# A two-layer mixer and mixture-of-experts block: the loop for left-over tokens moved behind the experts' first half, and a final norm from row sums

## Chip, cores and metric

The kernel runs on 1 core of one Trainium2 chip. The metric is the device time of one execution in microseconds (us), as the median of several runs. A program of one core has no other core to wait for, so the time is the length of its own longest chain of work.

## What is computed

Two layers over 256 latent tokens and 256 context tokens of width 1024. In each layer three token mixers (attention, gated linear attention, neighbourhood attention) are merged, added to the stream and normalised; then each token is routed to 2 of 32 experts, the experts' results are added to the stream, and it is normalised again. The second layer carries the 256 latent tokens alone through its experts. Cut to the part that the change touches:

```
def layer_norm(x, g, b):            # mean and variance over the 1024 columns
    return (x - mu) * rsqrt(var + 1e-6) * g + b

y = zeros(tokens, 1024)
for token, for its 2 experts e with gates a:     # SwiGLU experts, 1024 -> 512 -> 1024
    y[token] += a * (silu(h2[token] @ w1[e]) * (h2[token] @ w3[e])) @ w2[e]
x = layer_norm(alpha * x + gate2 * y, ln2_g, ln2_b)     # the "final norm" of the layer
# the next layer begins with
h = (x - mu(x)) * rsqrt(var(x) + 1e-6) * (1 + scale1) + shift1
```

All weights are float32. The experts' weights alone are 6 MB for each of 32 experts in each of 2 layers.

## The kernel before

**Layers and stages.** `run` goes through the layers. A layer's mixers work on tiles of 128 tokens by 1024 columns (four such tiles `x` in layer 0, and for its last part two in layer 1). Then the experts run (`experts`), then a loop for left-over tokens (`overflow`), then the final norm (`final_norm`), and in layer 1 the stream is stored. Layer 1 begins with `norm_T`, which normalises the four tiles, transposes them on TensorE and splits them into a high and a low part (`hThi`, `hTlo`) for the projections; the first of these is the small product `aT`, the next the projections `pT`.

**Experts.** Token places are set out in halves of 128 rows. A half serves one expert (H), two with 64 rows each (M) or four with 32 rows each (Q): layer 0 has 14 halves in the order MQHMQHMQHMQHMM, layer 1 has 16 halves of kind M. Two halves form a pair `dp`. `front(dp)` builds one-hot matrices for a pair on VectorE (lines 1361, 1362) and gathers its tokens on TensorE (line 1384, then the gates in lines 1369 and 1371). `body` multiplies a half by w1 and w3 (line 1507), `tail` applies silu and gate (lines 1403, 1404), transposes (1407), multiplies by w2 (1415), and after the second half of a pair calls `combine`, which brings the results back to token order on TensorE (1429, 1430), multiplies them by `g2` on VectorE (1432) and adds them to the stream (1433). The order is body 0, front 1, body 1, tail 0, body 2, tail 1, front 2 and so on.

**Weights.** An expert's weights are six pieces of 1 MB, four for `body` and two for `tail`. `load` requests them on SP's queue in the order of use and takes buffers in turn: 9 buffers in layer 0 (1 `pre`, 6 `ew`, 2 `ewb`), 14 in layer 1 (6 `ew`, 4 made of spare tiles, 4 `ewb`). A request waits on SP until the buffer's last reader is done.

**Left-over tokens.** Where an expert has more tokens than its rows, `overflow` serves them in blocks of 128 in a loop whose count, `nblk`, is known on the chip alone. With these inputs it is zero in both layers: no instruction of the loop's body is in the trace. All five engines still read the count, skip the body and meet at the loop's end. The instructions of this meeting stand in the profile under line 1546; there every engine goes through waits on the counters of the other engines and of all transfers that were requested ahead of the loop.

**Order of instructions.** A scheduler orders the instructions of each stretch between loops by priority, which is their place in the program: an engine takes the first ready instruction, and a later one where the earlier isn't ready. It can't move anything across a loop. So the program before has three stretches: to the end of layer 0's experts, from there to the end of layer 1's experts, and the last norm.

Of the kernel before, what the change touches and what calls it, by code (L numbers as in the profile page):

```python
# [21 lines left out]
NL = 2  # L22
NE = 32
# [226 lines left out]
class _Prog:  # L250
# [281 lines left out]
    def norm_T(self, l, xs):  # L532

        nc = self.nc
        xh = []
        for a in range(0, 4, NT[l]):
            for t, (_, r, m) in enumerate(self.stats_all(xs[a:a + NT[l]], APN[l]), a):
                h = self.t([128, 1024], ("whi", "wlo")[t % 2] if l else "g4", name="xh")
# [860 lines left out]
    def expert_tail(self, h1, h3, gate, w2, halves, end=False):  # L1399
# [10 lines left out]
        for n in range(2):  # L1410
            y = self.ps("Y")
            m = 128 // halves
            order = [(f, i) for f in range(4) for i in range(halves)]
            for f, i in sorted(order, key=lambda x: x[1]) if end else order:
                mm(y[m * i:m * i + m, :], aT[:, 128 * f + m * i:128 * f + m * i + m], w2(f, n, i), start=f == 0, stop=f == 3)  # L1415
            ns = slice(512 * n, 512 * n + 512)
            self.split2(y, Yh[:, ns], Yl[:, ns])
        return Yh, Yl

    def combine(self, CY, T, last):  # L1420

        nc, mm = self.nc, self.nc.tensor.matmul
        for n in range(2):
            for t in range(T):
# [8 lines left out]
                (nc.vector if last and n else nc.gpsimd).tensor_tensor(self.x1[t][:, ns], self.x1[t][:, ns], tmp, op=ALU.add)  # L1433
# [10 lines left out]
    def load(self, l, us, n, js, step=2048, most=99, after=None):  # L1444
# [4 lines left out]
        for j in js:  # L1449
            for i in range(len(us)):  # L1450
# [7 lines left out]
                if n < 6 or n >= 6 + extra:  # L1458
# [4 lines left out]
                    for v in range(0, 2048, step):  # L1463
                        self.nc.sync.dma_start(x[:, v:v + step], src[:, v:v + step])
                    w[i, j] = [x[:, 512 * v:512 * v + 512] for v in range(4)]
                else:
                    w[i, j] = []
                    for v, x in enumerate(self.spare[n - 6]):
                        self.nc.sync.dma_start(x, src[:, 1024 * v:1024 * v + 1024])
                        w[i, j] += [x[:, 0:512], x[:, 512:1024]]  # L1470

    def experts(self, l, T):
# [39 lines left out]
        def tail(dp, pr, us, hs):  # L1512
            end = SPL and 2 * dp + pr == len(halves) - 1
            self.load(l, us, 2 * dp + pr, (4,))
            self.load(l, us, 2 * dp + pr, (5,), 1024 if end else 2048)
            w = self.held[2 * dp + pr]
            Y = self.expert_tail(hs[0], hs[1], gates[dp][:, pr:pr + 1],
                                 lambda f, n, i: w[i, 4 + n][f], len(us), end)
# [8 lines left out]
        for n, x in enumerate(halves):  # L1527
            if x[1] == 1 and x[0] + 1 < len(gs):
                front(x[0] + 1)
            with self.later(0 if n else FIRST):  # L1530
                held[n] = body(*x)
            if n:
                tail(*halves[n - 1], held[n - 1])
        tail(*halves[-1], held[len(halves) - 1])
    def overflow(self, l, T):

# [4 lines left out]
        nc.vector.tensor_scalar(idx0, idx0, c["pcol"][:, 0:1], 6.0, op0=ALU.add, op1=ALU.mult)  # L1541
        if l:
            nc.vector.tensor_scalar(idx0, idx0, float(l * NE * 768), None, op0=ALU.add)
        table = self.a["ew"].rearrange("l e p j w -> (l e p j) w")
        nblk = nc.values_load(self.nblk[0:1, 0:1], min_val=0, max_val=16)
        with self.tc.For_i(0, nblk, 1):  # L1546
# [3 lines left out]
            w = []  # L1550
            for j in range(6):
                ii = self.small(1, I32)
                nc.vector.tensor_scalar(ii, row, float(j), None, op0=ALU.add)
                x = self.t([128, 2048], "ew", name="ow")
                nc.gpsimd.indirect_dma_start(out=x, out_offset=None, in_=table, in_offset=bass.IndirectOffsetOnAxis(ap=ii[:, :1], axis=0))
                w.append(x)
# [10 lines left out]
            for m in range(2):  # L1567
                h = self.ps("h")
                for k in range(8):
                    mm(h, XT[:, k], w[2 * m + k // 4][:, 512 * (k % 4):512 * (k % 4) + 512], start=k == 0, stop=k == 7)  # L1570
                hs.append(h)
            Y = self.expert_tail(hs[0], hs[1], gate, lambda f, n, i: w[4 + n][:, 512 * f:512 * f + 512], 1)
            col = self.small(1)
            nc.vector.tensor_tensor(col, sel, c["pcol"][:, 0:1], op=ALU.add)
            self.combine([(self.spots(self.slot_rows(self.over, T), col, T),) + Y], T, False)
# [5 lines left out]
    def final_norm(self, l, T, lgb):  # L1581

        nc = self.nc
        x = self.x1
        g, b = lgb
        for a in range(0, T, NB[l]):
            ts = range(a, a + NB[l])
            for t, (mu, r, m) in zip(ts, self.stats_all([x[t] for t in ts], APF[l])):
                if t in FQ[l]:
                    nc.vector.scalar_tensor_tensor(x[t], x[t], mu, g, op0=ALU.subtract, op1=ALU.mult)  # L1590
                    for i in range(2):
                        s = slice(512 * i, 512 * i + 512)
                        nc.vector.scalar_tensor_tensor(x[t][:, s], x[t][:, s], r, b[:, s], op0=ALU.mult, op1=ALU.add)  # L1593
                        if l == NL - 1:
                            nc.sync.dma_start(self.out[0, 128 * t:128 * t + 128, s], x[t][:, s])
                else:
                    nc.scalar.activation(x[t], x[t], AF.Identity, bias=m, scale=r)
                    nc.vector.tensor_tensor(x[t], x[t], g, op=ALU.mult)
                    (nc.vector if t in FD else nc.gpsimd).tensor_tensor(x[t], x[t], b, op=ALU.add)
                if t < 2 and l < NL - 1:  # L1600
                    nc.sync.dma_start(self.x2[t], x[t])
        return x
# [12 lines left out]
    def run(self):  # L1615
# [7 lines left out]
        for l in range(NL):  # L1623
# [48 lines left out]
            if l:  # L1672
                lgb = self.final_loads(l)
            self.overflow(l, T)
            if l == 0:
# [4 lines left out]
                lgb = self.final_loads(l)  # L1680
            xs = self.final_norm(l, T, lgb)
# [30 lines left out]
```

## Time and profile before

| | |
|---|---|
| median of 3 runs | 2152.49 us (2150.43 to 2153.63) |
| the profiled execution, its own time | 2150.77 us |
| its span, first to last instruction | 2148.9 us |
| TensorE (PE) busy | 1973.0 us, 92% |
| VectorE (DVE) busy | 964.7 us, 45% |
| ScalarE (ACT) busy | 561.5 us, 26% |
| GpSimd (POOL) busy | 277.5 us, 13% |
| moved by DMA | 562.41 MB, mean 262 GB/s |
| mean granted TensorE clock | 0.969 |

Times in the views are us from the span's start. PE is the matmul row, PEld its weight loads; engine names with a q are the engines' queues, where branches, semaphores and transfer requests are processed. A float32 matmul stands in the trace as two records. In rows of the timeline the first number is the start, the second the length from the first to the last of the instructions that the row merges. "DMA share" is the busy share of the 16 DMA engines. Layer 0's experts use weights from about 697 to 1176, layer 1's from 1674 to 2122.

### The profile page before, as it was taken

The page shows a single profiled execution, that of the slowest core. Times are in us where ns is not written, and L with a number is a line of the kernel's source. Part 1 is how long each engine was busy: PE and PEld are TensorE (multiplying, and loading weights), DVE is VectorE, ACT ScalarE, POOL GpSimd, SP SyncE. Part 2 cuts the span into 40 slices and gives each one's busy share as a digit, 9 for nine tenths or more (in the row PEclk, how much of TensorE's full clock was granted, in tenths as well). Part 3 has the DMA queues.
Part 4 walks back from the last instruction along what each step waited for, and adds up shares of the span by engine and source line. Part 5 has one row for each costly group of instructions (what it writes and reads, how often), then busy time and mean ns, then how long its engine had stood idle before and what let it go on. Part 6 is the DMA issues. An engine that isn't in the chain of part 4 may idle for free. (4 is left out here: it accounts for less than half of the span.)

```text
span 2148.9 us, 28075 instructions
## 1 busy us (share of the span) xinstructions
PE 1973.0 (92%) x10749; PEld 1179.0 (55%) x10749; DVE 964.7 (45%) x2236; ACT 561.5 (26%) x992; POOL 277.5 (13%) x268
## 2 busy tenths in 40 slices
PE   6999999999998898989899598999996999999995
PEld 2676777767885353445253176887795433333331
DVE  4676765554487131222022766776658222221113
ACT  3453344443333000000010254444452111100000
POOL 1322100011100010111011222100020001000000
PEclk9999999999999999999999798999997999999998
DMA  8436222333328999999998723642466999999995
GB/s 300 160 118 220 69 69 70 94 99 120 99 91 321 400 420 420 372 385 420 420 369 367 276 84 116 197 127 85 140 210 253 401 421 422 422 422 422 421 422 224
DMA packets 113987, 562.41 MB, mean 262 GB/s; under 512 B 13302, under 2 KB 14838, under 8 KB 72120
## 3 DMA queue, kind: packets, MB, share of 16 engines
q1 hardware_dynamic: 113272, 558.85, 67.7%
q8 instruction: 87, 1.43, 0.3%
q10 hardware_dynamic: 576, 1.70, 0.2%
q14 instruction: 52, 0.43, 0.1%
HBM read 557.36 MB, written 3.15 MB: 261 GB/s over the span
## 5 line engine op out<-in xcount | busy, mean ns | idle before, releaser
L1507 PE MATMUL h<-ew,XT 128*64 128x512 f32 (+2 forms) x2048 | 479.0, 616 | 39.6 <-DMA ew<-in_ew_dram 39.5
L1507 PEld LDWEIGHTS h<-ew,XT 128*64 128x64 f32 (+2 forms) x2048 | 147.3, 136 | 325.7 <-issue 251.0
L1415 PE MATMUL Y<-ew,aT 128*64 128x512 f32 (+2 forms) x1024 | 250.4, 598 | 10.2 <-DMA ew<-in_ew_dram 7.8
L292 DVE TENSOR_TENSOR wlo<-raw,whi 128x1024 fp32r<-128x1024 f32 (+1 forms) x140 | 179.1, 1279 | 138.0 <-ACT whi L291 136.9
L1433 POOL TENSOR_TENSOR x<-x,ct 128x512 f32<-128x512 f32 x82 | 104.9, 1306 | 996.9 <-DVE ct L1432 873.7
L380 PE MATMUL pT<-hThi,whi 128*128 128x512 f32 (+1 forms) x576 | 204.0, 354 | 2.2 <-DVE zq L869 1.4
L291 ACT CAST whi<-raw 128x1024 fp32r<-128x1024 f32 (+1 forms) x140 | 145.4, 1039 | 223.4 <-PE pT L381 123.8
L382 PE MATMUL pT<-hThi,wlo 128*128 128x512 f32 (+1 forms) x576 | 203.2, 353 | 0.2 <-DVE wlo L292 0.2
L381 PE MATMUL pT<-hTlo,whi 128*128 128x512 f32 (+1 forms) x576 | 202.9, 352 | 0.0
L1404 DVE SCALAR_TENSOR_TENSOR act<-h,s,sl 128x512 f32<-128x512 f32 x30 | 22.5, 751 | 317.6 <-PE h L1507 263.9
L806 ACT CAST Yh<-Y 128x512 fp32r<-128x512 f32 x60 | 35.2, 586 | 467.7 <-PE Y L1415 467.7
L1415 PEld LDWEIGHTS Y<-ew,aT 128*64 128x64 f32 (+2 forms) x1024 | 75.5, 133 | 149.2 <-issue 123.8
L807 DVE TENSOR_TENSOR Yl<-Y,Yh 128x512 fp32r<-128x512 f32 x60 | 41.4, 690 | 252.8 <-ACT Yh L806 249.7
L380 PEld LDWEIGHTS pT<-hThi,whi 128*128 128x128 f32 x576 | 110.7, 192 | 23.8 <-issue 6.0
L382 PEld LDWEIGHTS pT<-hThi,wlo 128*128 128x128 f32 x576 | 110.7, 192 | 16.1 <-issue 2.6
L381 PEld LDWEIGHTS pT<-hTlo,whi 128*128 128x128 f32 x576 | 110.7, 192 | 14.3 <-issue 1.9
L380 PE MATMUL pM<-whi,hThi 128*128 128x512 f32 (+1 forms) x304 | 110.7, 369 | 3.6 <-ACT qTkT L645 1.9
L381 PE MATMUL pM<-wlo,hThi 128*128 128x512 f32 (+1 forms) x304 | 110.9, 365 | 0.0
L382 PE MATMUL pM<-whi,hTlo 128*128 128x512 f32 (+1 forms) x304 | 110.1, 364 | 0.0
L495 PE MATMUL mod<-wmod,sT 128*32 128x512 f32 x320 | 75.2, 636 | 22.5 <-DVE s L341 14.1
L1408 ACT COPY aT<-aT 128x512 f32<-128x512 f32 x30 | 17.6, 585 | 294.4 <-PE aT L1407 294.4
L1384 PE MATMUL XT<-OH,h2hi 128*128 128x256 f32 x352 | 88.6, 289 | 0.2 <-DVE OH L1362 0.2
(364 smaller groups left out, 3088.5 us busy)
## 6 DMA issues: line engine op xcount, KB each, us to landing
ew<-in_ew_dram SPq DMA_DIRECT2D x326, 1024.0 KB, 13.6
raw<-in_w_dram SPq DMA_DIRECT2D x145, 512.0 KB, 3.7
ew<-in_ew_dram SPq DMA_DIRECT2D x116, 512.0 KB, 13.5
wmod<-in_wmod_dram SPq DMA_DIRECT2D x96, 512.0 KB, 6.4
nb<-in_nb_dram SPq DMA_DIRECT2D x32, 256.0 KB, 3.8
g<-md SPq DMA_DIRECT2D x12, 256.0 KB, 7.3
row<-in_ln_dram SPq DMA_DIRECT2D x4, 512.0 KB, 5.3
lgb<-in_ln_dram SPq DMA_DIRECT2D x4, 512.0 KB, 12.2
```

Source lines behind the costliest of these rows:

```text
L291: self.nc.scalar.copy(hi, src)
L292: (eng or self.nc.vector).tensor_tensor(lo, src, hi.bitcast(F32), op=ALU.subtract)
L380: mm(out, lh, rh, start=start, stop=False)
L381: mm(out, lh, rl, start=False, stop=False)
L382: mm(out, ll, rh, start=False, stop=stop)
L495: nc.tensor.matmul(p[32 * j:32 * j + 32, :], self.sT[:, k, :], raws[j // 2][:, 512 * (j % 2):512 * (j % 2) + 512], start=k == 0, stop=k == 7)
L806: self.nc.scalar.copy(hi, src)
L807: self.nc.vector.tensor_tensor(lo, src, hi.bitcast(F32), op=ALU.subtract)
L1384: mm(p[:, w * j:w * j + w], self.h2s[t][part][:, 128 * k:128 * k + 128], OH[:, t], start=t == 0 and part == 0, stop=t == T - 1 and part == 1)
L1415: mm(y[m * i:m * i + m, :], aT[:, 128 * f + m * i:128 * f + m * i + m], w2(f, n, i), start=f == 0, stop=f == 3)
L1433: (nc.vector if last and n else nc.gpsimd).tensor_tensor(self.x1[t][:, ns], self.x1[t][:, ns], tmp, op=ALU.add)
L1507: mm(h[m * i:m * i + m, :], XTs[dp][:, k, 128 * pr + m * i:128 * pr + m * i + m], w[i, 2 * q + k // 4][k % 4], start=k == 0, stop=k == 7)
```

## The change

1. `overflow` is called inside `experts`, behind the first half's body and tail. Ahead of it stand new calls of `load` that request weights of halves 1 and 2, as many as there are buffers. `front(1)`, which is called in the same turn, now stands behind the loop. The order becomes body 0, tail 0, loop, front 1, body 1, body 2, tail 1 and so on.
2. The loop's body takes its weights in 24 pieces of 256 KB through the small `ct` buffers and no longer in six through `ew`.
3. The last half's w2 pieces, four in all, are requested in halves of 512 KB, the first halves of all four ahead of the second halves, and the w2 product no longer goes by expert first.
4. `combine` of the last pair adds on VectorE throughout (before: GpSimd for the first 512 columns, VectorE for the second) with an instruction that also returns the row sums.
5. `final_norm` takes the mean from these sums and the variance from a squaring pass on ScalarE, tile by tile, where it had bn_stats over two tiles at a time; all scaling is on VectorE. It passes on the row sums of its result, and `norm_T` of layer 1 does likewise.
6. `final_loads` (the norm's gain and offset) follows the experts in both layers.

```
         xh = []
-        for a in range(0, 4, NT[l]):
+        for t in range(4 if l else 0):
+            h, st = self.t([128, 1024], ("whi", "wlo")[t % 2], name="xh"), self.small(20)
+            nmu, v, m = (st[:, i:i + 1] for i in range(3))
+            nc.vector.tensor_scalar(nmu, self.total[t], -1.0 / 1024, None, op0=ALU.mult)
+            nc.scalar.activation(h, xs[t], AF.Square, bias=nmu, accum_out=v)
+            nc.vector.tensor_scalar(v, v, 1.0 / 1024, EPS, op0=ALU.mult, op1=ALU.add)
+            r = self.rsqrt(v, 1, st[:, 3:6])
+            nc.vector.tensor_tensor(m, nmu, r, op=ALU.mult)
+            nc.scalar.activation(h, xs[t], AF.Identity, bias=m, scale=r)
+            xh.append(h)
+        for a in range(0, 0 if l else 4, NT[l]):
...
-            order = [(f, i) for f in range(4) for i in range(halves)]
-            for f, i in sorted(order, key=lambda x: x[1]) if end else order:
+            for f, i in [(f, i) for f in range(4) for i in range(halves)]:
...
+        if last:
+            self.sums = [self.small(2) for _ in range(T)]
...
-                (nc.vector if last and n else nc.gpsimd).tensor_tensor(self.x1[t][:, ns], self.x1[t][:, ns], tmp, op=ALU.add)
+                if last:
+                    nc.vector.scalar_tensor_tensor(self.x1[t][:, ns], tmp, 1.0, self.x1[t][:, ns], op0=ALU.mult, op1=ALU.add, accum_out=self.sums[t][:, n:n + 1])
+                else:
+                    nc.gpsimd.tensor_tensor(self.x1[t][:, ns], self.x1[t][:, ns], tmp, op=ALU.add)
...
+            for _, x, src in sorted(parts, key=lambda y: y[0]) if step < 2048 else parts:
+                self.nc.sync.dma_start(x, src)
...
-            end = SPL and 2 * dp + pr == len(halves) - 1
-            self.load(l, us, 2 * dp + pr, (4,))
-            self.load(l, us, 2 * dp + pr, (5,), 1024 if end else 2048)
+            end = 2 * dp + pr == len(halves) - 1
+            self.load(l, us, 2 * dp + pr, (4, 5), 1024 if end else 2048)
...
         for n, x in enumerate(halves):
+            if n == 1:
+                tail(*halves[0], held[0])
+                free = PRE[l] + 6 + RNG[l] + len(self.spare) + 6 * len(halves[0][2])
+                for j in (1, 2):
+                    self.load(l, halves[j][2], j, range(4), most=free - self.nw)
+                self.overflow(l, T)
             if x[1] == 1 and x[0] + 1 < len(gs):
                 front(x[0] + 1)
-            with self.later(0 if n else FIRST):
-                held[n] = body(*x)
-            if n:
+            held[n] = body(*x)
+            if n > 1:
                 tail(*halves[n - 1], held[n - 1])
...
+        for t in range(T):
+            x, st = self.x1[t], self.small(20)
+            nmu, v = st[:, 0:1], st[:, 1:2]
+            nc.vector.tensor_scalar(nmu, self.sums[t][:, 0:1], self.sums[t][:, 1:2], -1.0 / 1024, op0=ALU.add, op1=ALU.mult)
+            nc.scalar.activation(junk[:, t % 2] if l else junk.rearrange("p a b -> p (a b)"), x, AF.Square, bias=nmu, accum_out=v)
+            nc.vector.tensor_scalar(v, v, 1.0 / 1024, EPS, op0=ALU.mult, op1=ALU.add)
+            r = self.rsqrt(v, 1, st[:, 3:6])
+            STT(x, x, nmu, g, op0=ALU.add, op1=ALU.mult)
+            if l == NL - 1:
+                for i in range(2):
+                    s = slice(512 * i, 512 * i + 512)
+                    STT(x[:, s], x[:, s], r, b[:, s], op0=ALU.mult, op1=ALU.add)
+                    nc.sync.dma_start(self.out[0, 128 * t:128 * t + 128, s], x[:, s])
+                continue
+            self.total.append(st[:, 6:7])
+            STT(x, x, r, b, op0=ALU.mult, op1=ALU.add, accum_out=st[:, 6:7])
...
             self.experts(l, T)
-            if l:
-                lgb = self.final_loads(l)
-            self.overflow(l, T)
             if l == 0:
                 right.close()
                 left.close()
                 self.pre.close()
                 left, right = self.mixers(1)
-                lgb = self.final_loads(l)
-            xs = self.final_norm(l, T, lgb)
+            xs = self.final_norm(l, T, self.final_loads(l))
```

## Rows read from the trace of the kernel before

**Rows 1.** Busy time by stretch: PE, PEld, DVE, ACT, POOL, clock, DMA share, GB/s

```profile
697.00:1176.00 479.00, 442.77 (x2231) 199.97 (x2227) 102.69 (x166) 38.14 (x66) 61.08 (x48) 0.98 0.98 401
1674.00:2122.00 448.00, 428.23 (x1960) 165.32 (x1956) 85.74 (x140) 43.13 (x76) 36.40 (x28) 1.00 1.01 419
```

**Rows 2.** Waits in layer 0's experts, 690 to 1190: total us, times, longest

```profile
PEld h L1507 <- DMA ew<-in_ew_dram: 58.1, 34, 3.5
```

**Rows 3.** Busy time by stretch, the seam between the layers, columns as in rows 1

```profile
1175.50:1195.00 19.50, 13.31 (x52) 6.34 (x48) 9.24 (x15) 1.17 (x2) 4.97 (x4) 0.96 0.02 6
1195.00:1235.00 40.00, 22.59 (x78) 6.08 (x79) 32.40 (x100) 14.04 (x17) 11.14 (x4) 0.68 0.97 368
```

**Rows 4.** Timeline from layer 0's last additions to layer 1's first products

```profile
1188.83 1.29 DVE L1432 TENSOR_TENSOR ct<-cb,g 128x512 f32<-128x512 f32 x2 [1.53 <-PE cb L1430]
...
1194.07 0.81 SPq L1612 DMA_DIRECT2D lgb<-in_ln_dram  x2
...
1195.34 4.84 DVE L336 BATCH_NORM_STATS2 s<-x 128x6 f32<-128x512 f32 x8 [1.62 <-issue]
...
1214.91 2.18 DVE L1599 TENSOR_TENSOR x<-x,lgb 128x1024 f32<-128x1024 f32 x1
...
1224.36 4.64 ACT L539 ACTIVATE xh<-x,s 128x1024 f32<-128x1024 f32 x4 [16.15 <-DVE s L346]
...
1243.17 0.68 DVE L292 TENSOR_TENSOR hTlo<-h,hThi 128x512 fp32r<-128x512 f32 x1
```

**Rows 5.** Timeline of the run's end

```profile
2108.71 3.65 PE L1415 MATMUL Y<-ew,aT 128*64 128x512 f32 x16 [1.32 <-DMA ew<-in_ew_dram]
...
2126.20 3.66 PE L1415 MATMUL Y<-ew,aT 128*64 128x512 f32 x12
...
2136.07 2.47 DVE L336 BATCH_NORM_STATS2 s<-x 128x6 f32<-128x512 f32 x4 [1.70 <-issue]
...
2143.21 2.73 DVE L1593 SCALAR_TENSOR_TENSOR x<-x,s,lgb 128x512 f32<-128x512 f32 x4
```

**Rows 6.** A pass of VectorE over one tile, ns

```profile
L1590 DVE SCALAR_TENSOR_TENSOR x<-x,s,lgb x2: 1267/1273/1279, 2138.7 to 2140.0; 128x1024 f32<-128x1024 f32 x2
```

**Rows 7.** Instructions of the loop's line, both layers: ns min/median/max, first and last start

```profile
L1546 DVEq EVENT_SEMAPHORE  x25: 21/50/50, 1193.8 to 2135.8; - x25
L1546 SPq EVENT_SEMAPHORE  x23: 27/28/5606, 1187.2 to 2134.5; - x23
L1546 PEldq COMPARE_BRANCH  x6: 70/182/325, 1188.0 to 2134.6; - x6
```

**Rows 8.** Busy time by stretch, the last weights, columns as in rows 1

```profile
2120.00:2125.00 5.00, 4.34 (x18) 1.28 (x19) 0.21 (x1) 0.59 (x1) 0.00 (x0) 1.00 0.31 126
```

**Rows 9.** Busy time by stretch of 2 us, layer 0, columns as in rows 1

```profile
682.00:684.00 2.00, 2.00 (x10) 1.81 (x9) 2.00 (x12) 0.00 (x0) 0.00 (x0) 0.50 1.03 415
...
696.00:698.00 2.00, 2.00 (x12) 0.71 (x10) 0.00 (x0) 0.00 (x0) 0.00 (x0) 1.00 0.46 78
718.00:720.00 2.00, 2.00 (x24) 0.60 (x20) 1.23 (x3) 0.00 (x0) 0.00 (x0) 1.00 0.26 45
720.00:722.00 2.00, 2.00 (x24) 0.55 (x17) 0.00 (x0) 0.00 (x0) 0.00 (x0) 1.00 0.80 287
```

**Rows 10.** Timeline of PE, layer 0, the gather between halves 0 and 1

```profile
706.39 0.39 PE L1384 MATMUL XT<-OH,h2hi 128*128 128x256 f32 x1
...
715.17 7.91 PE L1507 MATMUL h<-ew,XT 128*32 128x512 f32 x66
```

**Rows 11.** Timeline of DVE, one-hot matrices of four tiles

```profile
716.41 1.67 DVE L1362 SCALAR_TENSOR_TENSOR OH<-cst,s,O 128x256 fp32r<-128x256 f32 x4
```

**Rows 12.** Timeline of PE, layer 1, the gather between halves 0 and 1

```profile
1683.35 0.39 PE L1384 MATMUL XT<-OH,h2hi 128*128 128x256 f32 x1
...
1687.81 12.67 PE L1507 MATMUL h<-ew,XT 128*64 128x512 f32 x58
```

**Rows 13.** The page's transfer requests: KB each, us from issue to landing

```profile
raw<-in_w_dram SPq DMA_DIRECT2D x145, 512.0 KB, 3.7
```

More of the change, by code (lines that the diff above doesn't have):

```diff
@@ L535, in norm_T @@
         xh = []
-        for a in range(0, 4, NT[l]):
+        for t in range(4 if l else 0):
[9 more added lines that the diff above has]
+        for a in range(0, 0 if l else 4, NT[l]):
             for t, (_, r, m) in enumerate(self.stats_all(xs[a:a + NT[l]], APN[l]), a):
-                h = self.t([128, 1024], ("whi", "wlo")[t % 2] if l else "g4", name="xh")
+                h = self.t([128, 1024], "g4", name="xh")
                 nc.scalar.activation(h, xs[t], AF.Identity, bias=m, scale=r)
@@ L1397, in spots, with expert_tail @@
         return C
-    def expert_tail(self, h1, h3, gate, w2, halves, end=False):
+    def expert_tail(self, h1, h3, gate, w2, halves):
         nc, mm = self.nc, self.nc.tensor.matmul
@@ L1449, in load @@
         for j in js:
+            parts = []
             for i in range(len(us)):
@@ L1462, in load @@
                         self.nc.gpsimd.tensor_copy(x[0:32, 0:1], after[0:32, 0:1])
-                    for v in range(0, 2048, step):
-                        self.nc.sync.dma_start(x[:, v:v + step], src[:, v:v + step])
+                    parts += [(v // step, x[:, v:v + step], src[:, v:v + step]) for v in range(0, 2048, step)]
                     w[i, j] = [x[:, 512 * v:512 * v + 512] for v in range(4)]
@@ L1468, in load @@
                     for v, x in enumerate(self.spare[n - 6]):
-                        self.nc.sync.dma_start(x, src[:, 1024 * v:1024 * v + 1024])
+                        parts.append((v, x, src[:, 1024 * v:1024 * v + 1024]))
                         w[i, j] += [x[:, 0:512], x[:, 512:1024]]
+            for _, x, src in sorted(parts, key=lambda y: y[0]) if step < 2048 else parts:
+                self.nc.sync.dma_start(x, src)
     def experts(self, l, T):
@@ L1512, in tail @@
         def tail(dp, pr, us, hs):
-            end = SPL and 2 * dp + pr == len(halves) - 1
-            self.load(l, us, 2 * dp + pr, (4,))
-            self.load(l, us, 2 * dp + pr, (5,), 1024 if end else 2048)
+            end = 2 * dp + pr == len(halves) - 1
+            self.load(l, us, 2 * dp + pr, (4, 5), 1024 if end else 2048)
             w = self.held[2 * dp + pr]
             Y = self.expert_tail(hs[0], hs[1], gates[dp][:, pr:pr + 1],
-                                 lambda f, n, i: w[i, 4 + n][f], len(us), end)
+                                 lambda f, n, i: w[i, 4 + n][f], len(us))
             col = 2 * dp + pr
@@ L1540, in overflow @@
         nc.vector.tensor_scalar(idx0, self.eb, 128.0, None, op0=ALU.mult)
-        nc.vector.tensor_scalar(idx0, idx0, c["pcol"][:, 0:1], 6.0, op0=ALU.add, op1=ALU.mult)
+        nc.vector.tensor_scalar(idx0, idx0, c["pcol"][:, 0:1], 24.0, op0=ALU.add, op1=ALU.mult)
         if l:
-            nc.vector.tensor_scalar(idx0, idx0, float(l * NE * 768), None, op0=ALU.add)
-        table = self.a["ew"].rearrange("l e p j w -> (l e p j) w")
+            nc.vector.tensor_scalar(idx0, idx0, float(l * NE * 3072), None, op0=ALU.add)
+        table = self.a["ew"].rearrange("l e p j (v w) -> (l e p j v) w", w=512)
         nblk = nc.values_load(self.nblk[0:1, 0:1], min_val=0, max_val=16)
@@ L1549, in overflow, with piece @@
             nc.vector.scalar_tensor_tensor(eq, eq, 1.0, idx0, op0=ALU.mult, op1=ALU.mult, accum_out=row)
-            w = []
-            for j in range(6):
+            def piece(j):
                 ii = self.small(1, I32)
                 nc.vector.tensor_scalar(ii, row, float(j), None, op0=ALU.add)
-                x = self.t([128, 2048], "ew", name="ow")
+                x = self.t([128, 512], "ct", name="ow")
                 nc.gpsimd.indirect_dma_start(out=x, out_offset=None, in_=table, in_offset=bass.IndirectOffsetOnAxis(ap=ii[:, :1], axis=0))
-                w.append(x)
+                return x
             d = self.small(2 * T)
@@ L1569, in overflow @@
                 for k in range(8):
-                    mm(h, XT[:, k], w[2 * m + k // 4][:, 512 * (k % 4):512 * (k % 4) + 512], start=k == 0, stop=k == 7)
+                    mm(h, XT[:, k], piece(8 * m + k), start=k == 0, stop=k == 7)
                 hs.append(h)
[L1572 to L1575, printed above, removed]
+            Y = self.expert_tail(hs[0], hs[1], gate, lambda f, n, i: piece(16 + 4 * n + f), 1)
+            p = self.ps("row")
+            for t in range(T):
+                nc.tensor.transpose(p[:, 128 * t:128 * t + 128], OH[:, t].bitcast(F32), self.ident)
+            C = self.t([128, 128 * T], "o1", F32R, "C")
+            nc.vector.tensor_copy(C, p[:, :128 * T])
+            self.combine([(C,) + Y], T, False)
             nc.vector.tensor_scalar(cnt, cnt, 1.0, None, op0=ALU.add)
@@ L1583, in final_norm @@
         nc = self.nc
-        x = self.x1
+        STT = nc.vector.scalar_tensor_tensor
         g, b = lgb
[L1586 to L1601, printed above, removed]
@@ L1602, in final_norm @@
-        return x
+        self.total = []
+        if l:
+            junk = self.t([128, 2, 1024], "e8", name="junk")
+        else:
+            junk = self.t([128, 2, 512], "g4", name="junk")
+        for t in range(T):
+            x, st = self.x1[t], self.small(20)
[13 more added lines that the diff above has]
+            STT(x, x, r, b, op0=ALU.mult, op1=ALU.add, accum_out=st[:, 6:7])
+            if t < 2:
+                nc.sync.dma_start(self.x2[t], x)
@@ L1604, in final_loads @@
+        return self.x1
     def final_loads(self, l):
```

## The prediction

> **What bounds the kernel now.** I read the page first, for the balance of engines, then busy time by stretch, then the waits, and last the timeline at the three places that the change touches. The stretches show two stages in which transfers set the pace: while the experts run, the DMA engines are busy 0.98 of the time in layer 0 and all of it in layer 1, at 401 and 419 GB/s [rows 1]. At 419 GB/s a piece of 1 MB (1.049 million bytes) takes 2.5 us. TensorE looks busy there too, but in layer 0 it waited for weights 34 times, 58.1 us in all [rows 2], and the ends of its matmuls are modelled. So a time without transfers, while weights are still to come, delays the end by as much. It is otherwise between the layers: nothing moves from 1175.5 to 1195, as SP stands at the loop, and then 40 us pass at 368 GB/s in which PE has 22.6 us of work [rows 3]. There a chain of VectorE and ScalarE decides: last additions, loop, statistics, norm, statistics again, `xh`, transposes [rows 4]. At the run's end it is VectorE alone [rows 5].
>
> **What the change gives back: the seam between the layers.** Before, from the first multiplication of the last additions at 1188.83 to the last `hTlo` at 1243.85 it takes 55.0 us, with 1.62 us at the loop and 4.84 us of bn_stats on the way [rows 4]. After, VectorE has for each tile a multiplication (1.29/2 = 0.65 us [rows 4]) and an addition with row sum (2.73 us for the four passes over 512 columns [rows 5], the last to its end 0.75, and some 0.07 to read the sum, an estimate), twice two passes at 1.27 us [rows 6] less their overlap (1.2 us apart), and some ten small instructions at 0.1 to 0.2 us: 1.5 + 2.5 + 1.3 = 5.3 us, for four tiles 21 us, so the last tile leaves the final norm at about 1210. Then `norm_T` needs of it a squaring pass on ScalarE (a pass over 1024 columns took 4.64/4 = 1.16 us [rows 4]), ten dependent small instructions (2 us) and the pass to `xh` (1.16): 1214.5. VectorE also does the small instructions of the three earlier tiles and the evictions of the first two tiles' transposes meanwhile, for which I add 5.5 us (an estimate): 1220. From the last `xh` to the last `hTlo` it took 14.8 us before [rows 4] (1229.0 to 1243.85) for four tiles; two of them are through by now, so 7.4 us: 1227.4, which is 16 us earlier. I take 15. The bounds: 9 us if the transposes take all 14.8 us again, 22 if the 5.5 us find gaps. The modulation weights, which cost those 40 us, can now be requested while PE finishes, since SP no longer stands at the loop (it waited 5606 ns there for the last of the engines [rows 7]); they then cost the chain nothing. If they came as late as before, PE's products would still be in the way of the transposes, which is the lower bound again.
>
> **The run's end.** The last weights land at 2121.6 (0.31 of the stretch from 2120 [rows 8]), yet the last w2 product runs from 2126.20 to 2129.86 [rows 5], as it comes behind the first 512 columns' product and combine. With the second halves of all four pieces last, only half of a product of 3.65 us [rows 5] for each column half is left after landing; I put the end at 2125.5. Four multiplications with additions, now all on VectorE, take 5.9 us from 2126.3: 2132.2, against 2134.4 (1.70 us of idle time before 2136.07 [rows 5]). From there to the last instruction's end at 2145.94 it took 11.6 us: the loop 1.7, bn_stats 2.5, the rest 7.4. The two first fall away, and a squaring pass comes in, of which little shows for the first tile and 1.3 us for the second, while the last additions' order leaves less to wait for: about 7.5 us, so 2139.7. That is 6 us; bounds 3 (products in the old order) and 8. In layer 0 the new order of the last requests gives nothing, as PE has 13.3 us of work after the last landing [rows 3]. GpSimd's additions of the first 512 columns, which VectorE takes over, fall into a stretch in which it is busy for 9.24 of 19.5 us [rows 3].
>
> **What the change costs: the loop in the middle of the weights.** The body isn't run, so its smaller pieces cost nothing. But every engine goes through waits at the loop's exit, some eleven in a loop (25 on VectorE for two loops [rows 7]), and they name the counters of all transfers requested ahead of it. Before, all weights had landed by then, and the price was 1.6 to 1.7 us [rows 4, 5]. Now nine requests in layer 0 and fourteen in layer 1 are made just ahead of the loop, and the loop ends when the last of them has landed. The stream itself isn't held until then; but at that moment every buffer is full, nothing is requested, and PE must first empty a buffer.
>
> Layer 0: transfers resume at about 697 when body 0 frees buffers [rows 9]. Three pieces of half 0 and nine more follow, 12 x 2.5 = 30 us, so the last lands at 727. Its buffer is free in time: body 0 is done at 706.4 [rows 10], silu and transposes take about 3 us, the two w2 products 2 x 3.65 us [rows 5], so 717, where the last two transfers need theirs at 722. PE then idles from 717 to the exit at 728. Queued behind the loop is first `front(1)`, by priority, then body 1. The first one-hot matrix is ready 0.9 us later (0.42 us [rows 11], as much before it). Before, the same work, from the gather's start at 706.39 [rows 10] to the transfers' return at 720.4 (share 0.26, then 0.80 [rows 9]), took 14.0 us. PE's clock comes on top: after a stretch of little work it was granted 0.50, the 1.2 GHz level, at 682 to 684 [rows 9]; four such us cost 2. So transfers resume at 745 and 18 us are lost, against 1.9 lost at the same place before [rows 9]: 16 us.
>
> Layer 1: transfers run without a gap from 1674 [rows 1]. Behind the fourteen that are there, twelve follow: the last lands at 1704, the exit is at 1705. One-hot 0.9, gather and gates 4.5 (1683.35 to 1687.81 [rows 12]), the first products, 3.65, that empty two buffers [rows 5], the clock 2, start of a transfer 0.7: 1716.7, so 13 us. After both gaps the stream goes on as before, and nothing makes the loss good: layer 1's stream has no other gap [rows 1], and layer 0's next half of four experts waits for weights anyway.
>
> The sum: 2150.77 (the profiled execution's own time, 1.7 under the median of 2152.49) + 16 + 13 - 15 - 6 = 2158.8; I say 2159.
>
> **A rule against the change.** PE's branches at the loop took 325 ns at most [rows 7], so I add nothing for the jump over the body. The Trainium skill (Runtime: NRT & Kernel Launch, section Instruction fetch mechanics) says that a taken branch whose target lies outside the instructions held has to wait until they are fetched by DMA. The trace doesn't bear this out with a long wait at the two loops of before. As a rival: a fetch at the exit in each layer on PE, priced like a small transfer on a quiet queue, 3.7 us [rows 13], gives 2159 + 7 = 2166.
>
> **Rivals.** (a) PE takes body 1 first and the gather later. Body 1's weights are ready, the one-hot matrices aren't, and an engine takes what is ready; against it, the gather went first in both layers before [rows 10, 12]. Then the gap ends after 3.65 + 2 + 0.7 us: 735 and 1711.4, a loss of 6 and 7.4, and the time is 2150.8 + 13.4 - 21 = 2143. It decides as soon as the two gaps together stay under 21 us. (b) The loop does not hold for the requested weights. The stream then covers the loop, PE's idle time is a few us of what it waits for anyway, and the time is about 2150.8 - 21 + 2 = 2132. Only the program's list of waits speaks against it, since nothing was in flight at the loops of before. (c) The seam gives nothing, because layer 1's start depends on something else than the last `xh`: 2159 + 15 = 2174. Against it: PE sat without work in front of the transposes, and ScalarE waited 16.15 us for the statistics [rows 4].
>
> **How the numbers follow.** Forecast 0.55, (a) 0.25, (b) 0.08, the jump 0.07, (c) 0.05. A difference under 0.2%, 4.3 us, is about what a measurement of this kernel can't tell from none. The forecast's own range is 2150 to 2167, from the bounds of its four terms; of its 0.55 some 0.37 lie above 2156.8 and 0.04 below 2148.2. From (a) 0.19 is faster and 0.05 the same, (b) is faster, the jump and (c) are slower. Faster 0.31, same 0.18, slower 0.51. The range for 8 in 10 leaves out (b), (c) and the tails: 2140 to 2167.
>
> **What would show it.** In the changed trace: PE idle for about 11 us after tail 0 in both layers, and no transfers for 13 to 18 us after it; line 1384 ahead of line 1507 behind the loop; semaphore waits of the loop's line that end with a landing. At the seam the modulation weights before 1195 and the first `aT` product some 15 us sooner, counted from the last addition. At the end no bn_stats. The forecast is wrong if transfers go on through the loop, if line 1507 comes first, or if the seam's chain is shortened by another amount than 9 to 22 us.

## The result, and the profile after

The changed kernel takes 2165.97 us (median of 4 runs, 2163.87 to 2168.70), the kernel before on the same chip 2151.46 us: ratio 1.0068, 95% interval 1.0050 to 1.0085, so slower by 14.5 us. The forecast was 2159, slower by 8. The profiled execution of after has a span of 2164.2 us, 15.3 more than that of before.

The table divides both spans at the same events. Landings and resumptions are read from stretches of 1 us by their DMA share, the rest from the timeline. A landing stands where the summed share ends, so the last few packets come up to 1.5 us later than its number. Each kernel has one profiled execution, which can lie some us off its median (7.2 us above it for e5_five_held).

| Stage | before | after | difference |
|---|---|---|---|
| to the transfers' return at half 0, layer 0 | 697.0 | 695.5 | -1.5 |
| from there to layer 0's last landing | 478.4 | 499.3 | +20.9 |
| to the end of layer 0's last combine on PE | 14.0 | 11.4 | -2.6 |
| to layer 1's first `pT` product | 60.9 | 47.1 | -13.8 |
| to body 0 of layer 1 | 419.1 | 419.8 | +0.7 |
| to layer 1's last landing | 451.9 | 467.3 | +15.4 |
| to VectorE's last instruction | 24.6 | 20.5 | -4.1 |

The two streams lose 36.3 us; the seam, the run's end and a shorter rest of work behind layer 0's last landing give back 20.5. The stretches of after around the loop show where the two lost (columns as in [rows 1]); layer 0's answer to [rows 9]:

```profile
714.00:716.00 2.00, 0.55 (x4) 0.00 (x0) 0.69 (x1) 0.59 (x1) 0.00 (x0) 1.00 0.99 414
...
726.00:728.00 2.00, 0.00 (x0) 0.00 (x0) 0.00 (x0) 0.00 (x0) 0.00 (x0) 0.50 0.28 115
728.00:730.00 2.00, 0.04 (x1) 0.05 (x1) 0.24 (x4) 0.00 (x0) 0.00 (x0) 0.50 0.00 0
...
744.00:746.00 2.00, 2.00 (x24) 0.65 (x20) 1.59 (x5) 0.00 (x0) 0.00 (x0) 1.00 0.00 0
746.00:748.00 2.00, 2.00 (x24) 0.65 (x20) 0.00 (x0) 0.00 (x0) 0.00 (x0) 1.00 0.35 74
...
1708.00:1710.00 2.00, 0.00 (x0) 0.00 (x0) 0.00 (x0) 0.00 (x0) 0.00 (x0) 0.50 0.34 143
1710.00:1712.00 2.00, 0.84 (x2) 0.75 (x3) 0.78 (x6) 0.00 (x0) 0.00 (x0) 0.50 0.00 0
1720.00:1722.00 2.00, 2.00 (x12) 0.68 (x10) 0.43 (x2) 0.00 (x0) 0.00 (x0) 1.00 0.00 0
1722.00:1724.00 2.00, 2.00 (x12) 0.61 (x10) 0.00 (x0) 0.00 (x0) 0.00 (x0) 1.00 0.40 61
```

PE is done with tail 0 at 714.6 and stands, while the transfers run on until 726.6 (0.28 of the stretch from 726, summed); they come back at 747.3. In layer 1 the last landing is at 1708.7, the return at 1723. Added up by their shares, the gaps cost 20.6 and 14.5 us. The instructions of the loop's line (1570 in after; first and last start) put the loop's end between landing and return, in layer 0 first, then in layer 1:

```profile
L1570 SPq EVENT_SEMAPHORE  x12: 28/28/28, 715.9 to 729.2; - x12
L1570 PEldq COMPARE_BRANCH  x3: 104/185/6066, 710.8 to 729.7; - x3
...
L1570 SPq EVENT_SEMAPHORE  x12: 28/28/28, 1698.9 to 1710.6; - x12
L1570 PEldq COMPARE_BRANCH  x3: 70/173/412, 1692.5 to 1710.9; - x3
```

SP passes its last wait at 729.2 and at 1710.6, 2.6 and 1.9 us behind the landings as the share sums them. Much of that is the stream's own end, which trickles. From 722 to 735, in 40 slices of 0.325 us, it is:

```profile
GB/s 429 454 429 429 454 429 429 403 378 403 454 378 353 126 76 76 76 25 25 0 0 0 0 0 0 0 0 0 0 25 0 0 0 0 0 0 0 0 0 0
```

The last packets of weights come at about 728.0 (the lone 25 is an instruction packet), in layer 1 at about 1709.7, so SP's last wait ends some 1 us behind them. The view of SP's waits from 712 to 735 puts 12.6 us at the loop's line down to landings of `ew`. PE's timeline behind the loop in layer 0:

```profile
729.96 0.79 PE L1440 MATMUL cb<-Yh,C 128*128 128x512 f32 x1 [15.41 <-DVE s L1503]
...
733.53 0.41 PE L1394 MATMUL XT<-OH,h2hi 128*128 128x256 f32 x1
...
742.68 3.64 PE L1525 MATMUL h<-ew,XT 128*32 128x512 f32 x32
```

Eight products of pair 0's combine come first (3.6 us, at granted clock 0.50), then the gather, and body 1 only 12.7 us behind the loop. The seam (the answer to [rows 4]):

```profile
1199.82 1.29 DVE L1443 TENSOR_TENSOR ct<-cb,g 128x512 f32<-128x512 f32 x2 [1.84 <-PE cb L1441]
...
1202.30 0.34 SPq L1648 DMA_DIRECT2D lgb<-in_ln_dram  x1
...
1203.67 17.54 SPq L493 DMA_DIRECT2D wmod<-in_wmod_dram  x10
...
1205.10 1.09 PE L1441 MATMUL cb<-Yl,C 128*128 128x512 f32 x4
...
1205.53 1.29 DVE L1443 TENSOR_TENSOR ct<-cb,g 128x512 f32<-128x512 f32 x2 [0.19 <-PE cb L1441]
...
1225.55 1.27 DVE L1635 SCALAR_TENSOR_TENSOR x<-x,s,lgb 128x1024 f32<-128x1024 f32 x1
...
1230.00 4.63 ACT L544 ACTIVATE xh<-x,s 128x1024 f32<-128x1024 f32 x4 [1.46 <-DVE s L281]
...
1244.85 2.36 DVE L292 TENSOR_TENSOR hTlo<-h,hThi 128x512 fp32r<-128x512 f32 x2
```

The row at 1199.82 is the first multiplication of the first 512 columns, the one at 1205.53 of the second; the row at 1188.83 in [rows 4] is of the second too. SP requests the norm's rows 3.9 us ahead of the last combine's end (1206.2); before it was 4.7 us behind it. From that end the last pass of the final norm takes 20.6 us to finish, the last `xh` 28.4 and the last `hTlo` 41.0, where it was 54.4.

### The profile page after: what moved, and what is told of

Read it like the earlier page. It is cut to its first block, busy times and chain, and to the rows that moved or that the text cites. A ratio compares the mean times of both kernels' runs of the same rounds, so it can differ in the third digit from the quotient of the medians.

```text
span 2164.2 us, 28127 instructions
## 1 busy us (share of the span) xinstructions
PE 1968.4 (91%) x10749; PEld 1180.1 (55%) x10749; DVE 960.3 (44%) x2275; ACT 569.4 (26%) x1008; POOL 260.2 (12%) x259
## 4 chain that ended last, share of the span: by engine, by line
PE 47%; DMA 15%; DVE 3%; ACT 2%; issue 1%; SPq 0%; DVEq 0%; ACTq 0%
DMA ew<-in_ew_dram 14%; PE h L1525 13%; PE Y L1424 9%; PE XT L1394 4%; PE cb L1440 2%; PE pT L380 2%; PE cb L1441 2%; PE pT L381 2%; PE pT L382 2%; PE pM L381 1%; PE pM L382 1%; PE pM L380 1%; PE PV L969 1%; PE PT L955 1%; PE S L1020 1%
## 5 line engine op out<-in xcount | busy, mean ns | idle before, releaser
L1424 PE MATMUL Y<-ew,aT 128*64 128x512 f32 (+2 forms) x1024 | 249.0, 598 | 11.4 <-DMA ew<-in_ew_dram 7.8
L1448 POOL TENSOR_TENSOR x<-x,ct 128x512 f32<-128x512 f32 x76 | 97.5, 1311 | 974.9 <-DVE ct L1443 974.9
L1414 DVE SCALAR_TENSOR_TENSOR act<-h,s,sl 128x512 f32<-128x512 f32 x30 | 22.5, 751 | 331.9 <-PE h L1525 277.0
L1440 PE MATMUL cb<-Yh,C 128*128 128x512 f32 x176 | 63.5, 435 | 36.4 <-DVE s L1503 30.2
## 6 DMA issues: line engine op xcount, KB each, us to landing
lgb<-in_ln_dram SPq DMA_DIRECT2D x4, 512.0 KB, 13.8
```

The lines of the kernel that those rows point to most:

```text
L1440: mm(p, C[:, 128 * t:128 * t + 128], Yh[:, ns], start=i == 0, stop=False)
L1448: nc.gpsimd.tensor_tensor(self.x1[t][:, ns], self.x1[t][:, ns], tmp, op=ALU.add)
```

## The experiments

All times are medians, ratios are to the kernel before run on the same chip in the same set, with 95% intervals. The stage times in the text are those of the table above, read from each kernel's profile.

**e1_loop_back.** The loop behind the experts, and with it body 1 ahead of tail 0 and no requests ahead of the loop; in layer 1 the norm's rows are requested ahead of it, as before. Everything else is as changed.

```diff
-            if n == 1:
-                tail(*halves[0], held[0])
-                ...
-                self.overflow(l, T)
...
-            if n > 1:
+            if n:
                 tail(*halves[n - 1], held[n - 1])
...
             self.experts(l, T)
+            if l:
+                lgb = self.final_loads(l)
+            self.overflow(l, T)
...
```

> The loop for left-over tokens stands behind the experts again, body 1 comes ahead of tail 0 and the requests ahead of the loop are gone; row sums, final norm and the order of the last requests stay as changed (the row sums leave out what the loop would add; no token is left over with these inputs). Theory: the loop in the middle of the weights cost 18.8 us of the transfers in layer 0 and 15.2 in layer 1 by the trace of the changed kernel, and its return costs some 5 us at the seam and 1.7 at the end: 2166 - 34 + 6.7 = 2139, at any rate 2134 to 2145. Rival (the row sums and the request order cost the time, not the loop's place): 2155 or more.

Measured 2136.79 us, 0.9937 (0.9914 to 0.9960). The two streams take 481.8 and 452.1 us (before 478.4 and 451.9), the seam's stage 49.3, the end 22.5. Most of the 3.4 us that layer 0's stream has more than before it has less behind the last landing (11.7 us to the last combine's end instead of 14.0). The theory holds and the rival falls: the loop's place, with the order and the requests that go with it, turns a gain of 0.6% into a loss of 0.7%.

**e2_five_less.** `free` is smaller by five in each layer.

```diff
-                free = PRE[l] + 6 + RNG[l] + len(self.spare) + 6 * len(halves[0][2])
+                free = PRE[l] + 6 + RNG[l] + len(self.spare) + 6 * len(halves[0][2]) - 5
```

> As the changed kernel, but five pieces fewer are requested ahead of the loop in each layer, so that the last one requested lands about when TensorE is done with tail 0 (714.6 and 1697). Theory (the exit waits for the landing of all that was requested ahead of it): the loop ends at about 717 and 1699, some 13 and 12 us sooner; SP then requests the other five while TensorE gathers, and of the gaps of 20.7 and 14.1 us about 7 and 3 are left: 2166 - 25 = 2141, 2137 to 2150. Rival (the loop's place costs by its joining of all engines, the fetch of instructions or the clock, whatever is in flight): ten pieces of 2.5 us come later, 2166 to 2190.

Measured 2163.16 us, 1.0057 (1.0037 to 1.0077), as the changed kernel. The experiment tells nothing of the theory: the same nine and fourteen requests go out ahead of the loop. In layer 0 SP makes twelve, three of half 0 and nine more, from 690.5 to 711.0 and the next at 741.8; in the changed kernel twelve from 694.9 to 715.5 and the next at 746.3. So the requests of body 1, which stand behind the loop in the source, moved up past it: that nothing is moved across a loop, as the section on the kernel before has it, doesn't hold for these requests. The last landings (722.0 and 1701.9) and the gaps (some 21 and 15.6 us) are those of after.

**e3_no_loop.** As e1_loop_back, without the call of `overflow` (tokens left over, of which there are none here, would get no service).

> The loop is left out altogether (no service for left-over tokens; there are none with these inputs), body 1 ahead of tail 0 as before, the rest as changed. Theory: what is left of e1_loop_back's time without 1.7 us at the end and 1.6 to 6 us at the seam: 2131 to 2136. Rival (loops cost next to nothing wherever they stand): within 2 us of e1_loop_back.

Measured 2141.10 us, 0.9949 (0.9932 to 0.9967). This lies outside both ranges. The theory's small print fell: without any loop the seam takes 49.2 us (49.3 with it) and the end 22.5 (22.5), so behind the experts the loop costs nothing that shows, with a new norm whose sums don't wait for it. The median is 4.3 us above that of e1_loop_back, but the intervals overlap, so that the two aren't told apart. In the profiled executions layer 1's stream takes 456.5 us instead of 452.1; the same 350 us of e1_loop_back, and then of e3_no_loop:

```profile
1740.00:2090.00 350.00, 330.95 (x1494) 124.74 (x1490) 67.58 (x108) 32.97 (x58) 31.24 (x24) 1.00 1.02 422
```

```profile
1740.00:2090.00 350.00, 329.58 (x1482) 124.55 (x1484) 67.57 (x108) 32.93 (x58) 31.20 (x24) 1.00 1.02 417
```

The queues are as full, but move 417 GB/s instead of 422, which over 450 us is 5 us. Why, and whether another execution of the same kernel would do so, no run here shows.

**e4_old_norm.** As changed, with the last additions, the statistics by bn_stats and the final norm of before (`combine`, `final_norm`, `norm_T`).

> As the changed kernel, with the loop in the middle and the requests ahead of it, but with the old last additions, bn_stats and final norm. Theory: the seam's gain of 13.4 us is two thirds the norm's and a third the loop's absence, and at the run's end the norm is worth 2: 2166 + 9 + 2 = 2177, 2172 to 2182. Rival (the seam gained because SP's requests no longer stand behind the loop): 2166 to 2170.

Measured 2174.95 us, 1.0111 (1.0092 to 1.0129), as the theory had it. The seam's stage takes 56.2 us: going from before over this kernel to the changed one, 4.7 of 60.9 us fall without the new norm and another 9.1 with it. At the run's end it is 21.4 against 20.5. VectorE's timeline shows what fell away at the seam:

```profile
1218.11 8.95 DVE L1611 TENSOR_TENSOR x<-x,lgb 128x1024 f32<-128x1024 f32 x4 [1.04 <-ACT x L1610]
1226.99 1.27 DVE L336 BATCH_NORM_STATS2 s<-x 128x6 f32<-128x512 f32 x2
```

**e5_five_held.** As changed, five requests made to depend on the loop (`cnt` is the loop's counter, `after` makes GpSimd write the buffer's first column from it ahead of the request).

```diff
                 for j in (1, 2):
-                    self.load(l, halves[j][2], j, range(4), most=free - self.nw)
+                    self.load(l, halves[j][2], j, range(4), most=max(0, free - 5 - self.nw))
                 self.overflow(l, T)
+                for j in (1, 2):
+                    self.load(l, halves[j][2], j, range(4), most=max(0, free - self.nw), after=self.cnt)
```

> As the changed kernel, with five of the requests really held behind the loop in each layer: their buffers' first element is written by GpSimd from the loop's counter, so that nothing can move them ahead (in e2_five_less the program's order put nine and fourteen ahead of the loop all the same). Theory (the exit waits for the landing of what was requested ahead of it): last landing before the loop at about 714 and 1696, loop ends at 717 and 1699 instead of 730 and 1711, the gaps of 20.7 and 14.1 us in the transfers shrink to about 7 and 3: 2166 - 25 = 2141, 2136 to 2150. Rival (joining all engines, instruction fetch, clock: the price does not hang on what is in flight): the exits stay where they are or the held pieces come 25 us later, 2166 to 2190.

Measured 2144.71 us, 0.9970 (0.9959 to 0.9982), 21 us less than the changed kernel, with the same work. SP's last waits at the loop, in layer 0 and in layer 1, and PE's branches:

```profile
L1575 SPq EVENT_SEMAPHORE  x12: 27/28/2999, 708.2 to 718.3; - x12
L1575 PEldq COMPARE_BRANCH  x3: 100/193/3694, 713.0 to 722.1; - x3
...
L1575 SPq EVENT_SEMAPHORE  x12: 28/28/2095, 1683.5 to 1693.7; - x12
L1575 PEldq COMPARE_BRANCH  x3: 70/181/409, 1688.2 to 1694.1; - x3
```

Counted from the transfers' return at half 0 the loop lets SP go after 20.3 us, instead of 33.7 in the changed kernel. In layer 0 two gaps are left, in the stretches of 2 us:

```profile
716.00:718.00 2.00, 0.76 (x4) 0.00 (x0) 0.58 (x1) 0.58 (x1) 0.00 (x0) 1.00 0.13 45
718.00:720.00 2.00, 0.00 (x0) 0.00 (x0) 0.18 (x2) 0.00 (x0) 0.65 (x5) 1.00 0.18 29
...
734.00:736.00 2.00, 2.00 (x29) 1.38 (x31) 0.87 (x5) 0.58 (x1) 0.00 (x0) 1.00 0.04 12
736.00:738.00 2.00, 2.00 (x24) 0.56 (x20) 1.92 (x6) 0.00 (x0) 0.00 (x0) 1.00 0.00 0
```

They cost 3.4 and 6.8 us, the second because PE still gathers when the five pieces have landed. Layer 1's costs 3.0 us.

**e6_all_held.** The same with every request of body 1 and later held behind the loop.

> The same with every request behind half 0's own held until the loop has ended. Theory: TensorE's tail 0 then sets the exit, at about 717 and 1699. In layer 0 the stream stops when half 0's last three pieces have landed (704.5) and goes on at 717: a gap of 12.5 us instead of 20.7. In layer 1 half 0's pieces have all landed at about 1674, and the gap is 25 us instead of 14.1: 2166 - 8 + 11 = 2169, 2163 to 2175. Rival (as for e5_five_held): the exits stay at 730 and 1711, gaps of 25 and 37 us, 2190 or more.

Measured 2170.90 us, 1.0104 (1.0087 to 1.0121). Now SP waits at the loop for the engines, in layer 0 for 10.8 us, in layer 1 for 26.2 us (the largest of its waits); the view of waits names VectorE, whose last work of tail 0 in layer 0 ends at 713.8, behind PE's last product at 712.4:

```profile
L1575 SPq EVENT_SEMAPHORE  x12: 28/28/10764, 697.0 to 714.0; - x12
...
L1575 SPq EVENT_SEMAPHORE  x6: 27/28/26232, 1662.4 to 1689.1; - x6
```

The gaps cost 13.7 and 29.1 us (expected 12.5 and 25). With e5_five_held and the changed kernel this makes three settings of one quantity, and the loop's end follows the later of two events in each: the last landing (the changed kernel), or the engines' end of tail 0 (here, and by a little in e5_five_held, where the last packets come at 716.7 and VectorE ends at 718.1).

**e7_layer1_only.** The loop in the middle in layer 1 only.

```diff
-            if n == 1:
+            if n == 1 and l:
```

> The loop in the middle in layer 1 only, behind the experts in layer 0 (whose row sums leave out what the loop would add; no token is left over); norm and request order as changed. Theory: e1_loop_back's 2137 plus the 15.2 us of layer 1's gap, less about 2 at the run's end: 2150, 2146 to 2154. Rival (what the second layer costs is only the delay of the first, handed on): 2137 to 2140.

Measured 2153.35 us, 1.0011 (1.0000 to 1.0022). Layer 1's stream takes 468.2 us, layer 0's 479.8: the two losses stand side by side and add up.

**e8_sums_in_loop.** As e1_loop_back, with the loop's additions writing the row sums too.

```diff
-            self.combine([(C,) + Y], T, False)
+            self.combine([(C,) + Y], T, True)
```

> As e1_loop_back, with the loop's own additions writing the row sums again, so that the norm is right with left-over tokens too. Theory: the loop's body is not entered, so this costs nothing: 2137, 2133 to 2141, faster than both kernels. Rival (the sums now wait for the loop, and the loop's exit costs the norm's start): 2141 to 2145.

Measured 2140.01 us, 0.9942 (0.9928 to 0.9955): within the range and faster than both kernels, with the service for left-over tokens complete in the program (none are left over, so it isn't exercised). But it isn't free: the trace has the rival's wait. The seam takes 50.3 us and the end 24.1, 1.0 and 1.6 more than in e1_loop_back. At the end VectorE is done with the last addition at 2126.6 and reads the row sums only behind the loop:

```profile
2128.28 0.34 DVE L1617 TENSOR_SCALAR s<-s 128x1 f32<-128x1 f32 x2 [1.71 <-issue]
```

**e9_body_first.** As changed, `front(1)` called behind body 1.

> As the changed kernel, but the second pair's gather and gates are called behind body 1, so that TensorE starts on body 1 when the loop ends. Theory (the transfers stand until TensorE has emptied a buffer, and in the changed kernel the first products of the combine and the gather go ahead of that): the transfers resume some 6.4 us behind the loop's end in each layer (first products 3.65, clock 2, start 0.7) instead of 17.4 and 12, so 11 + 5.5 us less: 2149, 2145 to 2154. Rival (the wait for the landings is the whole price, what comes first behind the loop is hidden): 2162 or more.

Measured 2155.80 us, 1.0010 (0.9995 to 1.0025), 1.8 us above the range. PE's timeline behind the loop, and the stretches of the last landing and of the return:

```profile
731.96 6.26 PE L1525 MATMUL h<-ew,XT 128*32 128x512 f32 x32 [15.29 <-DVE s L1503]
738.15 0.50 PE L1440 MATMUL cb<-Yh,C 128*128 128x512 f32 x1
```

```profile
728.00:730.00 2.00, 0.00 (x0) 0.00 (x0) 0.00 (x0) 0.00 (x0) 0.00 (x0) 0.50 0.28 115
738.00:740.00 2.00, 2.00 (x12) 1.43 (x8) 0.00 (x0) 0.00 (x0) 0.00 (x0) 1.00 0.47 86
```

The gaps shrink from 20.6 and 14.5 us to 10.5 and 9.6, 15 us in all where 16.5 were expected; the seam and the end take 4.5 us longer than in the changed kernel (50.3 and 21.8 us). So what goes first behind the loop is worth 15 us of stream, and the wait for the landings keeps the rest. The changed kernel's 47.1 us at the seam are the shortest of all; other kernels with the new norm take 48.7 to 50.3 with the loop in the middle, and 49.2 to 50.3 with it behind the experts.

**e10_held_body_first.** e5_five_held with that order.

> e5_five_held with body 1 ahead of the second pair's gather and gates. Theory: of the gaps left in e5_five_held (3.4 and 6.8 us in layer 0, 3.0 in layer 1) the second falls away, as body 1 empties its buffers while the five held pieces land: 2145 - 7 = 2138, 2134 to 2142, level with the loop behind the experts and faster than both kernels. Rival (the stream doesn't set layer 0's time, so that a closed gap gives nothing): 2143 or more.

Measured 2139.36 us, 0.9939 (0.9921 to 0.9957). Layer 0's second gap is gone, and its stream takes 482.0 us instead of 489.0. A loop in the middle of the weights is thus as good as one behind them, if little is in flight when it is reached and the work that empties buffers comes first.

## Why the prediction was right in kind and short by 7 us

The sign, the two gaps and the order behind the loop came as forecast. Every one of the four terms was some 1 to 2.5 us too favourable, 7.8 us in all; with -1.5 and +0.7 of the table, which no term forecast, they are the difference between 2159 and 2166.

- **Layer 0, +16 forecast, +18.3 measured** (20.9 of the stream, less 2.6 that PE needed less behind the last landing; against e1_loop_back it is 17.5 less 0.3, so 17.2). The last landing was put at 727 and came at 726.6, as the share sums it. The term was mis-sized in the loop's end: 1 us behind the landing by the prediction, 3.4 in the trace, of which 1.4 go to the last packets and 2.0 from there to PE's first product at 729.96. From there to the transfers' return it took 17.4 us where 17 were put, and that is partly luck. The eight products of the combine, 2.1 us at full clock (738.15 to 740.21 in e9_body_first), were not in the sum; the 0.9 us of the first one-hot matrix, which was, ran beside them, the clock cost 1.9 us, and the 14.0 us of [rows 10, 9] took 13.4.
- **Layer 1, +13 forecast, +15.4 measured.** Again the loop's end (PE's first product 2.4 us behind the landing instead of 1, at 1711.15), a gap of 14.5 instead of 12.7, and another 1.0 us at the dip ahead of it, 2.4 us where before had 1.4. The landing came at 1708.7 instead of 1704, as the seam had handed on 3.7 us and the dip 1; this moved the gap and did not lengthen it.
- **The seam, -15 forecast, -13.8 measured**, within the bounds. Counted as the prediction does, from the first multiplication of the second 512 columns (1188.83 in before, 1205.53 in after), the chain takes 41.7 us instead of 55.0. The final norm took 21.3 us of it where 21 were put, and the last `xh` was there after 29.1 where 31.2 were put, as some of the 5.5 us found gaps. The step that was mis-sized is the last transposes: 12.6 us, not 7.4. How the gain divides isn't settled. Over e4_old_norm some 9 of it are the norm's and 4.7 come without it; but with the new norm the seam takes 49.3 us with a loop behind the experts and 49.2 without any, so that 11.7 are there by the norm and the loop's leaving gives nothing that shows. The 2.1 us by which after is shorter still no run explains.
- **The run's end, -6 forecast, -4.1 measured.** The step that failed is that the last w2 product hangs on the last landing, so that only half a product for each column half is left behind it. The diff was misread to begin with ("the second halves of all four pieces last", and likewise in the section on the change): the list of parts is made anew for each `j`, so the halves are in turn within each pair of pieces, and the pair of the second 512 columns comes last as a whole. But the order of requests decides nothing here. PE's last wait for weights ends at 2127.58 (in before at 2108.71 [rows 5]), long ahead of the last landing, and from there its products and those of the combine go on without another, for 20.1 us to the end of the last w2 product. In before, with the old order, it takes 21.15 us; in nine of the ten experiments, with the new order, 21.1, and in e2_five_less 20.1. So the new order gave 0.1 us, and the 1 us more in after goes with another sequence of PE's rows, whose cause no run shows. The timeline of after (the answer to [rows 5]):

```profile
2127.58 3.65 PE L1424 MATMUL Y<-ew,aT 128*64 128x512 f32 x16 [1.33 <-DMA ew<-in_ew_dram]
...
2141.01 3.65 PE L1424 MATMUL Y<-ew,aT 128*64 128x512 f32 x14
...
2145.71 1.94 PE L1424 MATMUL Y<-ew,aT 128*64 128x512 f32 x8
...
2152.34 1.15 ACT L1624 ACTIVATE junk<-x,s 128x1024 f32<-128x1024 f32 x1 [4.05 <-DVE s L1623]
...
2159.52 1.41 DVE L1631 SCALAR_TENSOR_TENSOR x<-x,s,lgb 128x512 f32<-128x512 f32 x2
```

  The last product ends at 2147.65, 7.3 us behind the last landing by the table, where 3.9 were put; from there to the end it took 13.3 us, 0.9 less than put.
- **The rivals.** (b) falls with the first trace: SP's waits at the loop end with landings. (c) falls with the seam. (a) is the order of e9_body_first, and its price of 2143 was too low: the gaps are then still 10.5 and 9.6 us, and the time is that of before, not a faster one.
- **The jump over the body.** The changed kernel has one branch of 6.07 us on PE in layer 0, from 714.8 to 720.9, which costs nothing there as the landing comes at 726.6; that the rival's 2166 is the measured time is chance. In e5_five_held it takes 3.69 us and is bare: SP leaves at 718.3, PE at 722.1. In layer 1 it is 0.41 us, and at before's loops at most 0.33 [rows 7]. The Trainium skill (Runtime: NRT & Kernel Launch, section Instruction fetch mechanics) says that a taken branch to instructions that aren't held waits for a DMA to bring them. Layer 0's branch agrees with it: while it runs, one packet of an instruction queue moves (0.02 MB, in the changed kernel and in e5_five_held), and bare it takes the 3.7 us at which the rival priced it. In layer 1 no such packet moves from 1692 to 1700. But at before's loop in layer 0 three such packets move from 1185 to 1195 without a long branch, so why layer 0 has the wait in the middle and not at its end stays open.

The -1.5 us are the time at which layer 0's stream comes back ahead of the loop, the sums and the norm; in the eleven changed kernels' profiles it lies between 691.3 and 699.4. Totals of single executions that differ by 4 us are therefore not told apart here. Stage times do better, but not to the last us: layer 1's stream differs by 4.4 us between e1_loop_back and e3_no_loop, which have the same work there.

## What to carry to other kernels

A hardware loop whose body never runs was not free in the middle of a stream: its end waited for every transfer requested ahead of it and for every engine, and the stream then stood until buffers were emptied again. Put it where nothing is in flight, or hold back so many requests that the last landing meets the engines' arrival, and let the work that empties buffers come first behind it. Requests that are written later in the source may stand ahead of the loop in the program, so read the queue's order before counting on it.

## What the runs showed of the hardware

A skipped loop's branch on PE in the middle of layer 0 took 5.95 to 6.09 us in four kernels whose queue was full (the changed one, e2_five_less, e4_old_norm, e9_body_first) and 3.55 to 3.69 us in three that held requests back (e5_five_held, e6_all_held, e10_held_body_first); in layer 1 it took 0.40 to 0.42 us. The weights' stream went at 422 GB/s in layer 1 in one trace and at 417 in another, with the queues equally full (share 1.02), over 350 us.
